# Two Strassen sums kept in PSUM over seven chunks, and another order of down products and up units

## The chip, the cores and the metric

The kernel runs on one core of one Trainium2 chip. The metric is the device time of one execution in microseconds (us), the median of the runs shown; the profile is of one further execution. TensorE does the matmuls, VectorE (DVE) and ScalarE (ACT) the elementwise work, GpSimd (POOL) and SyncE (SP) mostly issue DMAs.

## The reference

A hybrid decoder block over 256 tokens of width 2048 in float32: an mLSTM branch and a block-sparse attention branch from one projection, merged by gates, then a residual and a squared-ReLU MLP. The change touches only the MLP:

```python
hn = rmsnorm(x, norm_ffn_pre[l])
u = jnp.square(jax.nn.relu(jnp.einsum('bsd,df->bsf', hn, w_up[l])))   # 2048 -> 8192
y = jnp.einsum('bsf,fd->bsd', u, w_down[l])                           # 8192 -> 2048
x = x + rmsnorm(y, norm_ffn_post[l])
```

## The kernel before

**Splitting.** TensorE multiplies rounded float32 (`float32r`). Each weight unit (128x2048, 1 MB) is loaded and split into a high part `whi` (a ScalarE cast, line 169) and a remainder `wlo` (a DVE subtraction, line 170), in two halves of 128x1024. Four buffers of each exist, so two units. A product is three matmuls: high by high, high by low, low by high.

**The MLP.** The hidden width 8192 is taken in eight chunks (`NCH = 8`, j = 0 to 7) of 1024. An *up unit* (U, `up_step`, product `mm_feat_one`, lines 215 to 217) makes 128 hidden channels with 48 matmuls of 256 columns; `up_post` (line 760 and a square on ScalarE) evacuates it. Eight U fill a chunk. For the chunks 0 to 6 the down projection goes by Strassen-Winograd products: `group(j, p)` takes one half p of the output columns with seven *down products* (D, `mm_factor`, lines 226 to 232, 12 matmuls of 512 columns) named p1, q5, p6, p2, q7, q3, q4, always in this order. A chunk thus has 14 D, and between them stand the eight U of the next chunk. The order is the string in the diff, written by hand.

**What a D needs.** Its right factor is a weight block or a sum of blocks. For q5, p6 and q4 DVE forms a running sum of 128x2048 first (lines 859, 865 and 881) from blocks `r11, r12, r22, r21`; for q7 a GpSimd DMA adds r22 onto r12 (line 874). The sums live in the four `rawl` buffers, up units and r11 in the three `raw` buffers, all loaded by SP's queue in order. The left factor is a sum or difference of quarters of the hidden activations; `factors(j)` makes seven `xs` from them (lines 776, 777, 787, 792, 796, 800), four after the chunk's last U and one after each of the next three D.

**What a D leaves.** Its PSUM bank is added into SBUF accumulators by DVE (`add`, line 849; line 900 for q7); in chunk 0 the first write of an accumulator is a ScalarE copy (line 847). `v` takes p1 and p6; `y11`, `y12`, `y21`, `y22` take the others. Bank "a" holds p1, and p2 is accumulated on top of it; q3 goes on top of q5 in "e", q4 on top of q7 in "b"; p6 has "f". After chunk 6, `v` is combined into the y's (line 896). Five banks rotate for U and D (`acc_tile`), three others (`sm_tile`) serve small matmuls outside this stage.

**Steps.** The main loop writes the split of step i before the matmuls and the post of step i-1. A scheduler of the framework then fixes each engine's instruction order from its own timing estimates, and within an engine the order is static. Chunk 7 is done afterwards without Strassen (`down_step`, `hold_step`, `last_step`).

Of the kernel before, what the change touches and what calls it, by code (L numbers as in the profile page):

```python
# [19 lines left out]
ALU = mybir.AluOpType  # L20
# [15 lines left out]
NCH = DFF // FCH  # L36
# [49 lines left out]
def tile_hybrid_block(ctx, tc, xT, pos, pre, small, wa, wi, wo, wu, wd, wpost, out):  # L86
    nc = tc.nc
    V, S, G, PE = nc.vector, nc.scalar, nc.gpsimd, nc.tensor
# [17 lines left out]
    def acc_tile():  # L106
        return pacc.tile([P, 512], F32, name="acc", tag="acc")

    def sm_tile():
        return psm.tile([P, 512], F32, name="sm", tag="sm")  # L110
# [39 lines left out]
    def load(src):  # L150
        raw = raw_tile()
        nc.sync.dma_start(out=raw[:, 0:src.shape[1]], in_=src)
        return raw

    def split(raw, place=None, half=1024, pieces=1, between=None):
        parts = []
        for h in range(2):
            if place is None:
                hi = wp.tile([P, 1024], F32R, name="whi", tag="whi", bufs=4)
                lo = wp.tile([P, 1024], F32R, name="wlo", tag="wlo", bufs=4)  # L160
            else:
                hi, lo = place[:, h, 0], place[:, h, 1]
            n = half // pieces
            for i in range(pieces):
                if between:
                    between(h * pieces + i)
                s = slice(i * n, (i + 1) * n)
                r = raw[:, h * half + i * n:h * half + (i + 1) * n]
                S.copy(out=hi[:, s], in_=r)  # L169
                V.tensor_tensor(out=lo[:, s], in0=r, in1=hi[:, s].bitcast(F32), op=ALU.subtract)  # L170
            parts.append((hi, lo))
        return parts

    def wk(parts, k, n):
        per = 8 if n == P else 2
        hi, lo = parts[k // per]
        s = slice((k % per) * n, (k % per + 1) * n)
        return hi[:, s], lo[:, s]
# [42 lines left out]
    def mm_factor(acc, parts, f, start, stop, pinned=False, more=False):  # L221


        for k in range(4):
            hi, lo = wk(parts, k, 512)
            first = PE.matmul(out=acc, lhsT=f[:, k, 0], rhs=hi, start=start and k == 0,  # L226
                              stop=False, skip_group_check=more)
            if pinned:
                tc.keep_in_program_order(first)
            PE.matmul(out=acc, lhsT=f[:, k, 1], rhs=hi, start=False, stop=False,  # L230
                      skip_group_check=more)
            PE.matmul(out=acc, lhsT=f[:, k, 0], rhs=lo, start=False, stop=stop and k == 3,  # L232
                      skip_group_check=more)
# [433 lines left out]
    late = {}  # L667
# [88 lines left out]
    uh, xs, todo = {}, {}, []  # L756
# [73 lines left out]
    def wd_unit(j, e, v):  # L830
        return wd[8 * j + 2 * e + v]

    def long_raw():
        return pool["f"].tile([P, 2048], F32, name="rawl", tag="rawl", bufs=4)

    def group(j, p):

        e1, e2 = 2 * p, 2 * p + 1
        b11, b12, b21, b22 = (wd_unit(j, e, v) for v in range(2) for e in (e1, e2))
        y, v = late["y"], late["v"][:, p]  # L840
        y11, y12, y21, y22 = (y[:, h, e * 512:(e + 1) * 512] for h in range(2) for e in (e1, e2))
        r, acc = {}, {}

        def add(dst, a, op=ALU.add):
            if j == 0 and op == ALU.add and id(dst) not in seen:
                seen.add(id(dst))
                S.copy(out=dst, in_=a)
            else:
                V.tensor_tensor(out=dst, in0=dst, in1=a, op=op)
        seen = set()  # L850

        def w_b11():
            r["11"] = load(b11)
            return [split(r["11"])]

        def w_t1():
            r["12"], r["t"] = long_raw(), long_raw()
            nc.sync.dma_start(out=r["12"], in_=b12)
            V.tensor_tensor(out=r["t"], in0=r["11"], in1=r["12"], op=ALU.add)
            return [split(r["t"])]  # L860

        def w_t2():
            r["22"] = long_raw()
            nc.sync.dma_start(out=r["22"], in_=b22)
            V.tensor_tensor(out=r["t"], in0=r["t"], in1=r["22"], op=ALU.add)  # L865
            return [split(r["t"])]

        def w_b21():
            r["21"] = long_raw()
            nc.sync.dma_start(out=r["21"], in_=b21)  # L870
            return [split(r["21"])]

        def w_t3():
            nc.gpsimd.dma_start(out=r["12"], in_=b22, accum_op=ALU.add)
            return [split(r["12"])]

        def w_b22():
            return [split(r["22"])]

        def w_t4():  # L880
            V.tensor_tensor(out=r["t"], in0=r["t"], in1=r["21"], op=ALU.add)
            return [split(r["t"])]

        def step(name, w, bank, start, post):
            def mm(units):
                if start:
                    acc[bank] = acc_tile()
                mm_factor(acc[bank], units[0], xs[j, name], start, True, more=not start)

            def after():  # L890
                post(acc[bank])
                if todo:
                    todo.pop(0)()
                if j == NCH - 2 and name == "q4":
                    for dst, op in ((y12, ALU.subtract), (y21, ALU.add), (y22, ALU.subtract)):
                        V.tensor_tensor(out=dst, in0=dst, in1=v, op=op)
            return w, mm, after

        def q7(a):
            V.tensor_tensor(out=y22, in0=y22, in1=a, op=ALU.subtract)  # L900
        return [step("p1", w_b11, "a", True, lambda a: add(v, a)),
                step("q5", w_t1, "e", True, lambda a: add(y22, a)),
                step("p6", w_t2, "f", True, lambda a: add(v, a)),
                step("p2", w_b21, "a", False, lambda a: add(y11, a)),
                step("q7", w_t3, "b", True, q7),
                step("q3", w_b22, "e", False, lambda a: add(y12, a)),
                step("q4", w_t4, "b", False, lambda a: add(y21, a))]
# [79 lines left out]
    def up_step(j, i):  # L987
        feat_step(wu[8 * j + i], hmov, lambda a: up_post(j, i, a), product=mm_feat_one)

    def down_group(j, p):  # L990

        made = []

        def part(n, what):
            def f(*a):
                if not made:
                    made.extend(group(j, p))
                x = made[n][what]
                if what == 0:
                    return x() if callable(x) else [split(load(u)) for u in x]  # L1000
                return x(*a)
            return f
        return [(part(n, 0), part(n, 1), part(n, 2)) for n in range(7)]
# [6 lines left out]
        up_step(0, i)  # L1010
    for j in range(NCH - 1):
        downs, i = down_group(j, 0) + down_group(j, 1), 0
        for what in "DUDUDDUDUDDUDUDDUDUDDD":
            if what == "D":
                steps.append(downs.pop(0))
            else:
                up_step(j + 1, i)
                i += 1
# [24 lines left out]
    units = {}  # L1043
# [100 lines left out]
```

## Time and profile before

| | before |
|---|---|
| median of 3 runs | 1436.42 us (1435.86 to 1437.91) |
| the profiled execution | 1436.87 us, span 1435.1 us |
| TensorE, DVE, ScalarE busy | 98%, 80%, 57% of the span |
| TensorE's granted clock | 0.997 of full speed |

The span goes from the first to the last instruction of the profile. A busy share says how much of it an engine executed; the ends of matmuls are modelled, so consecutive ones overlap in the records. An idle time is put down to the instruction whose semaphore came last.

### The profile page before, as it was taken

The page shows a single profiled execution, that of the slowest core. Times are in us where ns is not written, and L with a number is a line of the kernel's source. Part 1 is how long each engine was busy: PE and PEld are TensorE (multiplying, and loading weights), DVE is VectorE, ACT ScalarE, POOL GpSimd, SP SyncE. Part 2 cuts the span into 40 slices and gives each one's busy share as a digit, 9 for nine tenths or more (in the row PEclk, how much of TensorE's full clock was granted, in tenths as well). Part 3 has the DMA queues.
Part 4 walks back from the last instruction along what each step waited for, and adds up shares of the span by engine and source line. Part 5 has one row for each costly group of instructions (what it writes and reads, how often), then busy time and mean ns, then how long its engine had stood idle before and what let it go on. Part 6 is the DMA issues. An engine that isn't in the chain of part 4 may idle for free.

```text
span 1435.1 us, 21795 instructions
## 1 busy us (share of the span) xinstructions
PE 1410.6 (98%) x8570; PEld 1251.7 (87%) x8570; DVE 1147.5 (80%) x1607; ACT 815.2 (57%) x1200; POOL 17.3 (1%) x31
## 2 busy tenths in 40 slices
PE   8999999999999999999999999999999999999997
PEld 7988888888888888888899989989889898888975
DVE  7777766777676666665687899998999989999985
ACT  7655555565554445555656665565655655565561
POOL 0000000000000000000000000000000000000000
PEclk9999999999999999999999999999999999999998
DMA  8654444544455455554627665657646667655651
GB/s 255 222 182 176 162 171 178 184 177 174 175 184 198 178 190 190 180 202 176 249 77 251 236 217 171 261 185 262 232 152 239 225 209 246 216 195 195 239 201 59
DMA packets 44455, 282.45 MB, mean 197 GB/s; under 512 B 5116, under 2 KB 7424, under 8 KB 11712
## 3 DMA queue, kind: packets, MB, share of 16 engines
q1 hardware_dynamic: 41904, 265.57, 50.0%
q0 software_dynamic: 2304, 15.47, 5.8%
q8 instruction: 67, 1.10, 0.3%
q14 instruction: 36, 0.29, 0.1%
q10 hardware_dynamic: 144, 0.01, 0.0%
HBM read 278.93 MB, written 2.10 MB: 196 GB/s over the span
## 4 chain that ended last, share of the span: by engine, by line
PE 84%; DVE 11%; issue 2%; DMA 2%; ACT 1%; SPq 0%; DVEq 0%; ACTq 0%
PE acc L188 27%; PE acc L189 14%; PE acc L217 7%; PE acc L215 7%; PE acc L216 7%; DVE wlo L170 5%; PE acc L232 5%; PE acc L226 5%; PE acc L230 5%; PE acc L200 2%; PE acc L205 2%; DMA raw<-in_wa_dram 2%; PE acc L204 2%; DVE xs L777 1%; DVE rawl L865 1%
## 5 line engine op out<-in xcount | busy, mean ns | idle before, releaser
L169 ACT CAST whi<-raw 128x1024 fp32r<-128x1024 f32 (+2 forms) x420 | 424.9, 1016 | 418.9 <-PE acc L188 173.8
L170 DVE TENSOR_TENSOR wlo<-raw,whi 128x1024 fp32r<-128x1024 f32 (+2 forms) x420 | 495.2, 1182 | 207.2 <-ACT whi L169 197.5
L188 PE MATMUL acc<-xw,whi 128*128 128x512 f32 x1152 | 408.3, 395 | 0.0
L189 PE MATMUL acc<-xw,wlo 128*128 128x256 f32 x1152 | 328.6, 285 | 0.0
L217 PE MATMUL acc<-hw,wlo 128*128 128x256 f32 x992 | 279.7, 283 | 4.9 <-DVE wlo L170 4.9
L216 PE MATMUL acc<-hw,whi 128*128 128x256 f32 x992 | 279.0, 282 | 0.0
L215 PE MATMUL acc<-hw,whi 128*128 128x256 f32 x992 | 277.8, 282 | 0.0
L188 PEld LDWEIGHTS acc<-xw,whi 128*128 128x128 f32 x1152 | 216.4, 188 | 49.0 <-issue 0.4
L169 ACT CAST whi<-rawl 128x1024 fp32r<-128x1024 f32 x168 | 173.5, 1048 | 116.8 <-PE acc L216 52.1
L189 PEld LDWEIGHTS acc<-xw,wlo 128*128 128x128 f32 x1152 | 216.6, 188 | 0.9
L170 DVE TENSOR_TENSOR wlo<-rawl,whi 128x1024 fp32r<-128x1024 f32 x168 | 201.8, 1219 | 8.0 <-ACT whi L169 6.4
L217 PEld LDWEIGHTS acc<-hw,wlo 128*128 128x128 f32 x992 | 186.9, 188 | 9.9 <-DVE wlo L170 7.3
L215 PEld LDWEIGHTS acc<-hw,whi 128*128 128x128 f32 x992 | 186.0, 188 | 4.6 <-DVE t L760 0.2
L216 PEld LDWEIGHTS acc<-hw,whi 128*128 128x128 f32 x992 | 186.9, 188 | 2.0
L226 PE MATMUL acc<-whi,xs 128*128 128x512 f32 x440 | 174.7, 397 | 2.9 <-ACT whi L169 2.7
L232 PE MATMUL acc<-wlo,xs 128*128 128x512 f32 x440 | 172.3, 396 | 1.8 <-DVE wlo L170 1.8
L230 PE MATMUL acc<-whi,xs 128*128 128x512 f32 x440 | 173.9, 396 | 0.0
L232 PEld LDWEIGHTS acc<-wlo,xs 128*128 128x128 f32 x440 | 82.7, 188 | 20.9 <-DVE wlo L170 4.6
L226 PEld LDWEIGHTS acc<-whi,xs 128*128 128x128 f32 x440 | 82.7, 188 | 20.7 <-ACT whi L169 6.1
L230 PEld LDWEIGHTS acc<-whi,xs 128*128 128x128 f32 x440 | 82.7, 188 | 18.1
L188 PE MATMUL acc<-mg,whi 128*128 128x512 f32 x240 | 84.2, 393 | 0.0
L189 PE MATMUL acc<-mg,wlo 128*128 128x256 f32 x240 | 67.7, 283 | 0.0
(258 smaller groups left out, 1618.5 us busy)
## 6 DMA issues: line engine op xcount, KB each, us to landing
raw<-in_wi_dram SPq DMA_DIRECT2D x96, 1024.0 KB, 4.8
raw<-in_wu_dram SPq DMA_DIRECT2D x64, 1024.0 KB, 6.2
rawl<-in_wd_dram SPq DMA_DIRECT2D x42, 1024.0 KB, 8.2
raw<-in_wd_dram SPq DMA_DIRECT2D x22, 1024.0 KB, 4.9
raw<-in_wo_dram SPq DMA_DIRECT2D x16, 1024.0 KB, 4.8
rawl<-in_wd_dram POOLq DMA_DIRECT2D x14, 1024.0 KB, 10.7
raw<-in_wa_dram SPq DMA_DIRECT2D x8, 520.0 KB, 4.7
raw<-in_wa_dram SPq DMA_DIRECT2D x16, 256.0 KB, 5.0
```

The source lines that it names most:

```text
L169: S.copy(out=hi[:, s], in_=r)
L170: V.tensor_tensor(out=lo[:, s], in0=r, in1=hi[:, s].bitcast(F32), op=ALU.subtract)
L188: PE.matmul(out=accs[i][:, 0:2 * T], lhsT=hi, rhs=m, start=k == 0, stop=False)
L189: PE.matmul(out=accs[i][:, 0:T], lhsT=lo, rhs=m[:, 0, :], start=False, stop=k == nk - 1)
L200: first = PE.matmul(out=acc, lhsT=m[:, 0, ts], rhs=hi, start=start and k == 0, stop=False)
L204: PE.matmul(out=acc, lhsT=m[:, 1, ts], rhs=hi, start=False, stop=False)
L215: PE.matmul(out=acc, lhsT=hi, rhs=m[:, 0, :], start=k == 0, stop=False)
L216: PE.matmul(out=acc, lhsT=hi, rhs=m[:, 1, :], start=False, stop=False)
L217: PE.matmul(out=acc, lhsT=lo, rhs=m[:, 0, :], start=False, stop=k == KT - 1)
L226: first = PE.matmul(out=acc, lhsT=f[:, k, 0], rhs=hi, start=start and k == 0, stop=False, skip_group_check=more)
L230: PE.matmul(out=acc, lhsT=f[:, k, 1], rhs=hi, start=False, stop=False, skip_group_check=more)
L232: PE.matmul(out=acc, lhsT=f[:, k, 0], rhs=lo, start=False, stop=stop and k == 3, skip_group_check=more)
```

## The change

The products p1 and p6 get a PSUM bank per column half that is held from chunk 0 to chunk 6 and accumulates all seven products: three `sm_tile` banks and one `acc_tile` bank. Their additions into `v` go. In chunk 6 p1's bank is copied to `v`, and after p6 `v` is added to `y11` and p6's bank to `v`. p2 starts its own bank. The order string becomes another one with the same 14 D and 8 U.

```diff
         def step(name, w, bank, start, post):
             def mm(units):
+                if bank in ("p1", "p6"):
+
+                    if j == 0:
+                        late[bank, p] = sm_tile() if (bank, p) != ("p6", 1) else acc_tile()
+                    acc[bank] = late[bank, p]
+                    mm_factor(acc[bank], units[0], xs[j, name], j == 0, True, more=j > 0)
+                    return
                 if start:
                     acc[bank] = acc_tile()
                 mm_factor(acc[bank], units[0], xs[j, name], start, True, more=not start)
...
+        def last_p1(a):
+            if j == NCH - 2:
+                S.copy(out=v, in_=a)
+
+        def last_p6(a):
+            if j == NCH - 2:
+                V.tensor_tensor(out=y11, in0=y11, in1=v, op=ALU.add)
+                V.tensor_tensor(out=v, in0=v, in1=a, op=ALU.add)
+
         def q7(a):
             V.tensor_tensor(out=y22, in0=y22, in1=a, op=ALU.subtract)
-        return [step("p1", w_b11, "a", True, lambda a: add(v, a)),
+        return [step("p1", w_b11, "p1", True, last_p1),
                 step("q5", w_t1, "e", True, lambda a: add(y22, a)),
-                step("p6", w_t2, "f", True, lambda a: add(v, a)),
-                step("p2", w_b21, "a", False, lambda a: add(y11, a)),
+                step("p6", w_t2, "p6", True, last_p6),
+                step("p2", w_b21, "a", True, lambda a: add(y11, a)),
                 step("q7", w_t3, "b", True, q7),
...
-        for what in "DUDUDDUDUDDUDUDDUDUDDD":
+        for what in "DUDDUDUDDUDUDDUDUDDUDD":
```

## Rows read from the trace of the kernel before

**Rows 1.** The page, busy time of each engine, share of the span, instructions.
```profile
PE 1410.6 (98%) x8570; PEld 1251.7 (87%) x8570; DVE 1147.5 (80%) x1607; ACT 815.2 (57%) x1200; POOL 17.3 (1%) x31
```

**Rows 2.** Busy time by stretch, two MLP chunks; then granted clock, DMA share, GB/s.
```profile
945.00:1032.00 87.00, 85.58 (x554) 77.01 (x553) 82.12 (x84) 51.36 (x60) 1.71 (x2) 1.00 0.63 218
1119.00:1206.00 87.00, 85.59 (x554) 77.01 (x553) 82.12 (x84) 51.37 (x60) 1.72 (x2) 1.00 0.64 219
```

**Rows 3.** Waits from 900 to 1400: total us, times, longest.
```profile
ACT whi L169 <- DVE rawl L865: 38.4, 11, 4.0
...
PE acc L217 <- DVE wlo L170: 4.9, 5, 1.0
...
PE acc L226 <- ACT whi L169: 2.2, 5, 0.4
PE acc L232 <- DVE wlo L170: 1.8, 2, 1.3
```

**Rows 4.** Groups by line and form, 900 to 1400, then the tile `v`.
```profile
L170 DVE TENSOR_TENSOR wlo<-rawl,whi 128x1024 fp32r<-128x1024 f32 x132 | 158.6, 1219 | 6.4 <-ACT whi L169 4.8
L169 ACT CAST whi<-rawl 128x1024 fp32r<-128x1024 f32 x132 | 136.3, 1048 | 90.9 <-PE acc L216 38.7 <-DVE rawl L865 38.4 <-PE acc L230 10.1
L865 DVE TENSOR_TENSOR rawl<-rawl 128x2048 f32<-128x2048 f32 x11 | 25.1, 2285 | 0.0
L859 DVE TENSOR_TENSOR rawl<-raw,rawl 128x2048 f32<-128x2048 f32 x10 | 22.9, 2292 | 4.8 <-DMA raw<-in_wd_dram 4.1 <-DMA rawl<-in_wd_dram 0.6
L849 DVE TENSOR_TENSOR v<-v,acc x26: 675/680/685, 795.4 to 1359.0; 128x512 f32<-128x512 f32 x26
```

**Rows 5.** TensorE's timeline, 1052 to 1062: start, duration, line, idle before.
```profile
1052.10 0.40 PE L230 MATMUL acc<-whi,xs 128*128 128x512 f32 x1
...
1054.21 0.39 PE L230 MATMUL acc<-whi,xs 128*128 128x512 f32 x1
1055.57 0.39 PE L217 MATMUL acc<-hw,wlo 128*128 128x256 f32 x1 [0.97 <-DVE wlo L170]
1055.80 0.28 PE L215 MATMUL acc<-hw,whi 128*128 128x256 f32 x1
...
1061.02 0.28 PE L217 MATMUL acc<-hw,wlo 128*128 128x256 f32 x1
```

**Rows 6.** DVE's timeline over one chunk, 1052 to 1140.
```profile
1052.09 2.29 DVE L881 TENSOR_TENSOR rawl<-rawl 128x2048 f32<-128x2048 f32 x1
1054.30 1.22 DVE L170 TENSOR_TENSOR wlo<-raw,whi 128x1024 fp32r<-128x1024 f32 x1
...
1086.53 2.29 DVE L865 TENSOR_TENSOR rawl<-rawl 128x2048 f32<-128x2048 f32 x1
1089.24 0.42 DVE L760 SCALAR_TENSOR_TENSOR t<-acc,rbc 128x256 f32<-128x256 f32 x1 [0.43 <-PE acc L217]
1090.00 2.36 DVE L170 TENSOR_TENSOR wlo<-rawl,whi 128x1024 fp32r<-128x1024 f32 x2 [0.34 <-ACT whi L169]
...
1094.01 2.28 DVE L881 TENSOR_TENSOR rawl<-rawl 128x2048 f32<-128x2048 f32 x1
...
1106.15 2.29 DVE L859 TENSOR_TENSOR rawl<-raw,rawl 128x2048 f32<-128x2048 f32 x1
...
1109.50 0.42 DVE L760 SCALAR_TENSOR_TENSOR t<-acc,rbc 128x256 f32<-128x256 f32 x1
...
1125.91 1.22 DVE L170 TENSOR_TENSOR wlo<-rawl,whi 128x1024 fp32r<-128x1024 f32 x1
1127.05 0.69 DVE L800 TENSOR_TENSOR s_b<-s_b,u 128x512 f32<-128x512 f32 x1
...
1130.25 2.29 DVE L865 TENSOR_TENSOR rawl<-rawl 128x2048 f32<-128x2048 f32 x1
...
1139.13 2.29 DVE L881 TENSOR_TENSOR rawl<-rawl 128x2048 f32<-128x2048 f32 x1
```

**Rows 7.** Waits from 770 to 936, chunk 0 and most of chunk 1.
```profile
PE acc L226 <- ACT whi L169: 0.5, 2, 0.3
```

## The prediction

> **What bounds the kernel now.** I read the page first. TensorE is busy 98% of the span, VectorE (DVE) 80%, ScalarE 57% [rows 1], so the question is what little TensorE idles and where. The stretches of one MLP chunk each come next: in both shown TensorE is busy 85.6 of 87.0 us and DVE 82.1 [rows 2], at a granted clock of 1.00. So two engines are nearly full here, with DVE's share far above its mean. The waits between 900 and 1400 us say who keeps TensorE waiting: always a weight half that is not yet split, by DVE's `wlo` or ScalarE's `whi`, never a PSUM bank [rows 3]. I also note there how long ScalarE waits for the sum of line 865: 38.4 us in 11 times [rows 3].
>
> The reader should see a pipeline with little slack. A weight unit passes a cast (ScalarE), a subtract (DVE) and the matmuls, and only four halves (two units) of `whi` and `wlo` exist. DVE can thus be little more than one unit ahead of TensorE.
>
> **The floor.** In the PE timeline nine steps between starts of 512-column matmuls take 2.11 us, 0.234 each; 44 steps between 256-column ones take 5.22 us, 0.119 each [rows 5]. A down product (D, 12 matmuls) is 2.81 us, an up unit (U, 48) 5.69, a chunk (14 D, 8 U) 84.9. The same instruction (line 881, p = 0) starts at 1052.09 and 1139.13 [rows 6], a period of 87.04. So 2.1 us per chunk are lost, in two places: 1.0 us of idle before a U's `wlo` and 0.4 before a D's `whi`, five times each [rows 3], plus their shadows (an idle of 0.97 is a start 1.13 late, since the records' modelled ends overlap [rows 5]). Five chunks lose 10.7, the first two some 0.8 (0.5 of idle, [rows 7]), the end of the last chunk 2.1 (1.8 of idle at line 232, [rows 3]): 13.6 us. No better feeding of TensorE in this stage can give more.
>
> **The change part by part.**
>
> *Fewer sums.* The 26 DVE additions into `v` go [rows 4]; at 0.68 us each with 0.08 of overlap to the next, 0.60, that is 15.6 us. Added, both halves p together: two copies on ScalarE in place of the two that started `v`, and four DVE additions at 0.60. Net 13.2 us of DVE, 2.4 in each of chunks 1 to 5. This alone ends nothing: DVE isn't what TensorE waits for everywhere, only around two places. What counts is which of the additions stand ahead of a late weight. Of the p1 sum, one of p = 0 does (between `wlo` halves after the chunk's border), so 0.6 us is won there. For TensorE nothing changes: p2 starts a bank of its own instead of adding to p1's, in the same 12 matmuls. Held for seven chunks are the three spare banks and one of five rotating ones. The a, e, b banks and a U's are then the four in use; since no TensorE wait names a bank now [rows 3], I price this at nothing, with an upper bound under the rivals. ScalarE's count stays, in copies of the same size, at 57% busy [rows 1].
>
> *The order.* D and U counts stay. Before: D U D U DD U D U DD U D U DD U D U DDD, after: D U DD U D U DD U D U DD U D U DD U DD. At the border four D in a row become three. But p = 0's q5 and p6, which had a U between them, now stand side by side, right after that border (q3 q4 p1 U q5 p6). Both take a 2048-wide sum before they can be split (lines 859, 865: 2.3 us, [rows 4]). No DMA is added; loads move with their steps, and on SP's queue the ones of p6 and U swap.
>
> *What goes.* The 1.24 late at p = 0's U (idle 0.97 and shadows, [rows 5]) comes from line 881's sum, which stands ahead of that U's `wlo` (1052.09, then 1054.30, [rows 6]) while p6 and p2 were side by side. Afterwards p6 is followed by a U, whose cast is ready early, so I take this to go. The border's loss, the 0.9 left of the 2.1, falls with one D less in the run: 0.3 in my estimate, between 0 and 0.9.
>
> *What comes: the pair.* I count from the end of the chunk's last U (U7), which is the row of line 760 at 1109.50 before [rows 6]. TensorE then has q3, q4, p1 (8.4), U0 (5.7) and q5 (2.8): p6 starts at 16.9 and needs its first `wlo` 0.5 later, at 17.4. DVE, at that point, has split q3 and half of q4; line 881's sum of p = 1 and line 859's of the next chunk are done, as they were before (1094.01 and 1106.15, [rows 6]). DVE has left, start to start (0.08 below the durations, [rows 4, 6]): the U's own 0.33, a half of q4 1.13, p1, U0 and q5 2.27 each, two drains 1.2, and the seven 0.6 us operations of the factors which before's order put between 1109.50 and q5's second half at 1125.91 [rows 6]. Sum 13.7. Next before came a factor difference (line 800, 1127.05): 14.3. Then line 865 starts; from its start to the first subtract of its unit is 3.47 us where DVE was not in the way (1086.53 to 1090.00, [rows 6]: the sum 2.3, the cast 1.05, [rows 4]), and that subtract is 1.2: ready at 18.9. TensorE is 1.5 late. As a check, the pair of p = 1 exists before: line 865 there starts 2.7 us ahead of its U's end (1086.53, 1089.24, [rows 6]) and nothing stalls, with 1.3 to spare (first half ready at 1091.2, used at 1092.5 by the floor). Here it starts 0.2 after the U's end, 2.9 later in relation to it: 1.6 late.
>
> The bounds of this term: if four factor operations that aren't urgent come behind line 865, it starts 2.4 earlier and the pair costs 0. If all factors and U0's post come ahead (1.5 more), it costs 3.0. If line 859's sum is not done in time, 2.2 more, 5.2. The factors come earlier in the written order than p6's sum, which speaks for the upper order; before's rows show two of them behind it, which speaks for the lower. I take the middle of 1.5 and 3.0: 2.2 us.
>
> *Sum.* Six chunks at 2.2 and the first (no D run ahead) at 1.8: 15.0; six borders at 0.3: 1.8; the end, with two D instead of three after the last U, 1.5 (0 to 2.5): together 18.3 against 13.6. The change costs 4.7 us. The profiled execution is 1436.87, its span 1435.1 and 1.8 around it; it stands 0.45 above the median of the runs. 1436.4 + 4.7 = 1441.1.
>
> **The Trainium skill** (Perfetto Trace Analysis, Identifying the Most-Contended Engine) holds that relieving the engine with the highest occupancy improves a kernel. The trace agrees in part: DVE has 82.1 of 87.0 here [rows 2], but TensorE's floor is higher. By that rule alone each chunk would shorten to the floor. Its result is the first rival, priced from rows below.
>
> **Rivals.**
>
> 1. *The pair is hidden, and the relief counts.* DVE reaches line 865 two microseconds before U0's end, as in p = 1. For it: 2.4 us less DVE work per chunk and two bubbles' causes gone. Against: the count above leaves DVE no idle time from the border to there. Left over: borders 1.8, end 1.5, some 0.2 per chunk for small lags, 4.7 in all; 8.9 won, 1427.5. It decides if the pair costs under 1.1.
>
> 2. *An even trade.* Before's order of the factors holds, the pair costs 1.5 (first chunk 1.2): 10.2 + 3.3 = 13.5 against 13.6, 1436.3. The additions then only gave DVE idle time, so the change's first half would have done nothing that the end sees.
>
> 3. *Line 859 slips too.* The sum for q5 needs a slot and a 1 MB load; with p2 and q7 side by side the slot comes free earlier, but DVE is fuller there. The pair at 4.4 costs 13 more than forecast: 1454. A PSUM wait belongs here as well: four rotating banks instead of five. If each chunk had one matmul group wait for two drains (1.2), that would be 8.4 us, 1449.5 with the rest. The Trainium skill (Perfetto Trace Analysis, Optimization Strategy) reads a bubble that repeats as a possible lack of SBUF or PSUM for the next tile. By the rows the present ones are named after weights, so I give banks little.
>
> **Chances.** The forecast case (1439.3 to 1449) has 0.38, rival 3 0.08, rival 2 0.24, rival 1 0.30. This kernel's measurement tells some 0.2%, 2.9 us, from no change. Slower 0.46, same 0.24, faster 0.30. The range takes in rival 1's price down to 1428 and the upper order with a bad end: 1428 to 1452. The forecast case alone: 1439 to 1449.
>
> **What would show it.** Right: in the steady chunks, TensorE's wait of about 1 us before line 217 is gone; a new one appears at p6 of p = 0, released by ScalarE's `whi` or DVE's `wlo`, ScalarE idle before it on line 865; the chunk's period is 87.4, DVE's busy time in a chunk 2.7 lower (79.4). The additions to `v` fall to two. Wrong, if the period drops towards 85, if line 865's row of p = 0 starts before U0's post, or if a TensorE row names a DVE addition (a bank).

## The result and the profile after

The changed kernel takes 1460.29 us (median of 4 runs, 1459.72 to 1463.63) beside 1436.14 for the kernel before in the same comparison: a ratio of 1.0172, 95% interval 1.0153 to 1.0191. It is slower by 24 us, where 4.7 were forecast and the range ended at 1452. Its profiled execution is 1460.17 us, the span 1458.4.

The page of the changed kernel, busy time of each engine and, in tenths over 40 slices, TensorE's granted clock:

```profile
PE 1423.2 (98%) x8570; PEld 1262.1 (87%) x8570; DVE 1137.2 (78%) x1585; ACT 814.4 (56%) x1200; POOL 17.3 (1%) x31
...
PEclk9999999999999999999999999999999999999999
```

DVE lost 22 instructions and 10 us of work against [rows 1], as the change says, and TensorE, with the same 8570 matmuls, is busy 12.6 us longer. That second number is the odd one: a late weight makes idle time, not busy time. The tenths of the clock line are too coarse to say why.

The waits of the changed kernel from 770 to 1440 us (total, times, longest):

```profile
ACT xs L776 <- DVE s_b L800: 28.0, 6, 5.2
...
PE sm L226 <- ACT whi L169: 16.0, 7, 3.0
...
ACT whi L169 <- DVE rawl L865: 8.0, 6, 2.4
...
PE sm L232 <- DVE wlo L170: 5.4, 7, 1.1
...
PE acc L232 <- DVE wlo L170: 0.8, 1, 0.8
```

The wait of line 217 is gone from the list, as is that of line 226 on an "acc" bank [rows 3]. Instead TensorE waits in a product on an "sm" bank, once per chunk, first for a high half (2.3 us each) and then for a low one (0.8). Idle put down to waits is 22.2 us against 9.4 before [rows 3, 7], 12.8 more. That is about half of the 24 us.

TensorE's timeline at the place, in the chunk around 1140:

```profile
1138.55 0.28 PE L217 MATMUL acc<-hw,wlo 128*128 128x256 f32 x1
1138.66 0.40 PE L232 MATMUL acc<-wlo,xs 128*128 128x512 f32 x1
...
1140.76 0.40 PE L232 MATMUL acc<-wlo,xs 128*128 128x512 f32 x1
1143.51 0.51 PE L226 MATMUL sm<-whi,xs 128*128 128x512 f32 x1 [2.35 <-ACT whi L169]
1143.85 0.39 PE L230 MATMUL sm<-whi,xs 128*128 128x512 f32 x1
1145.31 0.79 PE L232 MATMUL sm<-wlo,xs 128*128 128x512 f32 x1 [1.07 <-DVE wlo L170]
1145.90 0.63 PE L226 MATMUL sm<-whi,xs 128*128 128x512 f32 x1
...
1146.76 0.63 PE L232 MATMUL sm<-wlo,xs 128*128 128x512 f32 x1
```

U0's last matmul starts at 1138.55, q5's rest follows, then p6 of p = 0 waits twice: 2.52 us between starts beyond the usual 0.234, then 1.23; with the 0.11 between them p6 is 3.85 us late. After it the starts are 0.43 apart instead of 0.234, with no wait named. The same stretch by windows (time, then busy time of TensorE, its weight loads, DVE, ScalarE, GpSimd, then granted clock, DMA share and GB/s):

```profile
983.92:1075.47 91.55, 88.17 (x553) 79.29 (x553) 80.07 (x80) 51.26 (x60) 1.71 (x3) 0.96 0.60 207
...
1140.00:1145.40 5.40, 1.98 (x8) 0.97 (x7) 5.40 (x7) 4.27 (x7) 0.00 (x0) 0.97 0.05 20
1145.40:1147.00 1.60, 1.60 (x4) 1.31 (x5) 1.60 (x2) 0.91 (x2) 0.00 (x0) 0.50 0.00 0
1147.00:1149.00 2.00, 2.00 (x8) 1.62 (x8) 2.00 (x3) 1.04 (x1) 0.00 (x0) 0.64 0.00 0
1149.00:1153.00 4.00, 4.00 (x32) 3.82 (x31) 4.00 (x3) 1.50 (x2) 0.00 (x0) 1.00 0.71 262
```

The granted clock is 0.50, the lower level of 1.2 GHz, right after the wait, in which TensorE had been busy 1.98 of 5.40 us, and 1.00 again by 1149. That is the added busy time. The first row is a whole chunk, from one GpSimd DMA issue of p = 0 to the next: 91.55 us where 87.4 were forecast, with DVE at 80.07.

DVE's timeline, from line 859's sum and U7's post to p6's weights:

```profile
1117.46 2.28 DVE L859 TENSOR_TENSOR rawl<-raw,rawl 128x2048 f32<-128x2048 f32 x1
...
1124.81 0.42 DVE L760 SCALAR_TENSOR_TENSOR t<-acc,rbc 128x256 f32<-128x256 f32 x1
1125.74 1.23 DVE L170 TENSOR_TENSOR wlo<-rawl,whi 128x1024 fp32r<-128x1024 f32 x1 [0.51 <-ACT whi L169]
...
1139.10 0.68 DVE L800 TENSOR_TENSOR s_b<-s_b,u 128x512 f32<-128x512 f32 x1
1139.70 0.42 DVE L760 SCALAR_TENSOR_TENSOR t<-acc,rbc 128x256 f32<-128x256 f32 x1
1140.04 2.28 DVE L865 TENSOR_TENSOR rawl<-rawl 128x2048 f32<-128x2048 f32 x1
1142.24 0.68 DVE L849 TENSOR_TENSOR y<-y,acc 128x512 f32<-128x512 f32 x1
1142.84 0.68 DVE L777 TENSOR_TENSOR xs<-s_b,xs 128x512 fp32r<-128x512 f32 x1
1143.44 0.68 DVE L777 TENSOR_TENSOR xs<-u,xs 128x512 fp32r<-128x512 f32 x1
1144.04 2.35 DVE L170 TENSOR_TENSOR wlo<-rawl,whi 128x1024 fp32r<-128x1024 f32 x2
```

Line 865 starts 1.4 us after U0's end, TensorE arrives at p6 at 1141.0, and ScalarE's cast of p6 can begin only at 1142.4. Behind the sum stand three small operations, then the subtract. ScalarE's timeline of the same stretch:

```profile
1139.82 0.62 ACT L776 CAST xs<-s_b 128x512 fp32r<-128x512 f32 x1 [5.12 <-DVE s_b L800]
...
1142.41 1.99 ACT L169 CAST whi<-rawl 128x1024 fp32r<-128x1024 f32 x2 [1.13 <-DVE rawl L865]
```

ScalarE stands for 5 us at a copy that waits for line 800, with p6's casts queued behind it. This is a second candidate for what is late (rival E below), and it needs an experiment, since after its copies ScalarE waits another 1.13 us, for line 865.

### The profile page after: what moved, and what is told of

Same layout as the page of the kernel before. It is cut to its first block, busy times and chain, and to the rows that moved or that the text cites. A ratio compares the mean times of both kernels' runs of the same rounds, so it can differ in the third digit from the quotient of the medians.

```text
span 1458.4 us, 21829 instructions
## 1 busy us (share of the span) xinstructions
PE 1423.2 (98%) x8570; PEld 1262.1 (87%) x8570; DVE 1137.2 (78%) x1585; ACT 814.4 (56%) x1200; POOL 17.3 (1%) x31
## 4 chain that ended last, share of the span: by engine, by line
PE 89%; DVE 7%; issue 2%; ACT 1%; DMA 1%; SPq 0%; DVEq 0%; ACTq 0%
PE acc L188 26%; PE acc L189 14%; PE acc L215 8%; PE acc L216 8%; PE acc L217 8%; PE acc L230 5%; PE acc L226 5%; PE acc L232 5%; DVE wlo L170 3%; PE acc L200 2%; PE acc L205 2%; PE acc L204 2%; PE sm L232 1%; DVE xs L777 1%; PE sm L226 1%
## 5 line engine op out<-in xcount | busy, mean ns | idle before, releaser
L230 PE MATMUL acc<-whi,xs 128*128 128x512 f32 x356 | 140.9, 396 | 0.0
L226 PE MATMUL acc<-whi,xs 128*128 128x512 f32 x356 | 140.7, 396 | 0.0
L232 PE MATMUL acc<-wlo,xs 128*128 128x512 f32 x356 | 138.0, 395 | 0.8 <-DVE wlo L170 0.8
L232 PEld LDWEIGHTS acc<-wlo,xs 128*128 128x128 f32 x356 | 66.9, 188 | 14.5 <-DVE wlo L170 1.3
L230 PEld LDWEIGHTS acc<-whi,xs 128*128 128x128 f32 x356 | 67.0, 188 | 14.0
L226 PEld LDWEIGHTS acc<-whi,xs 128*128 128x128 f32 x356 | 67.1, 188 | 11.7
```

## The experiments

**Theories.** *A*: q5 and p6 of p = 0 stand side by side behind the chunk's border, so line 865's sum is late; TensorE waits there, and a lower clock follows. *B*: the held PSUM banks cost the time. *C*: runs of D must be spread evenly. *D*: the slow steps after the wait are late halves, not the clock. *E*: ScalarE's blocked queue, not line 865, is late.

Each kernel below was timed beside the kernel before on the same chip; the ratio's 95% interval is in brackets.

**The order alone** (the kernel before with the new string):

```diff
-        for what in "DUDUDDUDUDDUDUDDUDUDDD":
+        for what in "DUDDUDUDDUDUDDUDUDDUDD":
```

> The new order string alone, the sums as before. Theory A (p = 0's q5 and p6 side by side behind the chunk's border: line 865's sum comes too late, TensorE waits 3.9 us there, and a lower clock for some us follows): as slow as the changed kernel or slower, since the addition of p1 stands in the same stretch again, 1460 to 1480 us. Rival B (the held PSUM banks cost the time): 1434 to 1440 us.

Measured: 1452.33 us, 1.0113 [1.0098, 1.0129]. The order alone gives two thirds of the loss, so B's number falls. A's lower bound of 1460 was missed too. Its waits, TensorE's alone, 770 to 1400:

```profile
PE acc L226 <- ACT whi L169: 14.1, 7, 2.4
PE acc L232 <- DVE wlo L170: 4.2, 8, 0.8
```

The same place, seven times, a little shorter than with the whole change (18.3 us of idle in all, for 22.2). So in this order the held sums didn't help but cost 8 us more; the run on the factors' place below says through what.

**The sums alone** (the changed kernel with the old string).

> The sums kept in PSUM, the old order string. Theory A: no pair there, 2.4 us less DVE work per chunk, but only what stands ahead of a late weight counts: 1429 to 1436 us. Rival B (held banks): 1450 us or more, TensorE rows that wait for DVE additions.

Measured: 1432.82 us, 0.9979 [0.9969, 0.9989]: 3 us faster. None of TensorE's waits is put down to an addition that empties a bank:

```profile
PE acc L217 <- DVE wlo L170: 2.9, 5, 1.1
PE acc L232 <- DVE wlo L170: 1.8, 2, 1.3
PE acc L226 <- ACT whi L169: 0.5, 2, 0.3
```

The forecast said that only additions ahead of a late weight would count. They do: 10.5 us less of DVE busy time (1137.0 against 1147.5 [rows 1]) bought 3, and the waits fell from 9.4 [rows 3, 7] to 5.2.

**The pair apart** (the changed kernel, q5 and p6 of p = 0 parted by a U again, still three D at the border):

```diff
-        for what in "DUDDUDUDDUDUDDUDUDDUDD":
+        for what in "DUDUDDUDUDDUDDUDUDDUDD":
```

> The changed kernel with the string D U D U DD U D U DD U DD U D U DD U DD: q5 and p6 of p = 0 apart again, still three D at the border. Theory A: no wait at p6 of p = 0, no lower clock, a chunk of 85.5 to 87 us, 1428 to 1438 us. Rival C (fewer U between the D near the border, whichever products they are): still over 1450 us. Rival B: still over 1450 us.

Measured: 1432.28 us, 0.9978 [0.9968, 0.9987]. B and C fall: same sums, same evenness, 28 us less. The wait at a late low half of a U is back:

```profile
PE acc L217 <- DVE wlo L170: 4.2, 5, 0.9
PE sm L226 <- ACT whi L169: 2.4, 5, 0.9
```

**One U moved** (the kernel before; a U goes from between q5 and p6 of p = 0 to between p6 and p2; the border's four D stay):

```diff
-        for what in "DUDUDDUDUDDUDUDDUDUDDD":
+        for what in "DUDDUDUDUDDUDUDDUDUDDD":
```

> The kernel before with one U moved, from between q5 and p6 of p = 0 to behind p6 and p2's place (D U DD U D U D U ..., four D at the border as before). Theory A: the pair stalls behind a border that is fuller still, 1460 to 1485 us. Rivals B and C (banks; evenness of the order): 1434 to 1442 us.

Measured: 1462.98 us, 1.0193 [1.0178, 1.0208]. One U in another place, without any other part of the change, is enough for the whole loss. Its waits at p6 are mostly 2.0 and 1.1 us of idle.

**The wait filled** (the changed kernel; the useless matmuls go into p2's bank, which p2 then starts anew):

```diff
                 if bank in ("p1", "p6"):
+                    if name == "p6" and p == 0 and j > 0:
+                        acc["a"] = acc_tile()
+                        hw = late["hw"]
+                        for _ in range(16):
+                            tc.keep_in_program_order(
+                                PE.matmul(out=acc["a"], lhsT=hw[:, 0, 0, 0:P], rhs=hw[:, 1],
+                                          start=True, stop=True))
...
-                if start:
+                if start and not (name == "p2" and p == 0 and j > 0):
                     acc[bank] = acc_tile()
```

> The changed kernel with 16 useless matmuls of 512 columns ahead of p6's of p = 0 in chunks 1 to 6, written into p2's bank before p2 starts it. Theory A with the clock: they fill the 3.8 us in which TensorE would wait (16 x 0.234), the granted clock stays at 1.00, and only the slow steps behind the wait (2.2 to 2.9 us a chunk) go: 1443 to 1448 us, the wait itself not won back. Rival D (the slow steps are matmuls that wait for late halves): 1457 to 1463 us.

Measured: 1449.07 us, 1.0091 [1.0076, 1.0106], a little above the forecast's 1448: 96 more matmuls, 11.2 us less than the changed kernel. Its windows around the same p6, the 16 matmuls in the first:

```profile
1136.00:1140.20 4.20, 4.20 (x20) 3.43 (x19) 4.20 (x5) 3.07 (x6) 0.00 (x0) 1.00 0.01 4
1140.20:1143.00 2.80, 2.76 (x13) 2.00 (x12) 2.80 (x3) 2.71 (x3) 0.00 (x0) 1.00 0.00 0
```

The granted clock stays at 1.00 and the slow steps are gone though the halves come no sooner (p6's first subtract starts 5.4 us after U0's end, 5.5 in the changed kernel): D falls. The matmuls took about as long as the wait (16 x 0.234 = 3.7), so some 11 us are what the lower clock costs, nearly 2 a chunk, and 12.8 of more waiting with 11.2 of clock come to the 24. The wait in chunk 0 was not filled, and the lower level follows it in this run.

**The last two factors later** (the changed kernel; DVE's order pinned so that line 865 stands ahead of line 800, and the last two factors follow p6's split):

```diff
-            V.tensor_tensor(out=t[2], in0=t[2], in1=a12, op=ALU.add)
+            tc.keep_in_program_order(
+                V.tensor_tensor(out=t[2], in0=t[2], in1=a12, op=ALU.add))
...
-            V.tensor_tensor(out=r["t"], in0=r["t"], in1=r["22"], op=ALU.add)
+            t2 = V.tensor_tensor(out=r["t"], in0=r["t"], in1=r["22"], op=ALU.add)
+            if p == 0:
+                tc.keep_in_program_order(t2)
...
-                if todo:
+                if todo and (len(todo) == 3 or name in ("p6", "p2")):
                     todo.pop(0)()
```

> The changed kernel with the last two factors (line 800's difference and two subtractions of line 777) put behind p6's split in DVE's order. Theory A: line 865 starts 0.6 us sooner and the first subtract behind it 1.2 to 1.8 us sooner; the wait at p6 falls from 3.8 to between 1.5 and 2.7 us and the low clock after it gets shorter or goes: 1445 to 1454 us. Rival C (evenness of the order) and B (banks): 1457 to 1463 us.

Measured: 1450.74 us, 1.0104 [1.0089, 1.0120], 9.5 us less than the changed kernel. Its waits at p6, TensorE's alone:

```profile
PE sm L226 <- ACT whi L169: 12.4, 7, 2.3
PE sm L232 <- DVE wlo L170: 3.7, 7, 0.5
```

They fall from 21.4 to 16.1 us; the rest of the gain is TensorE's busy time, 1418.2 for 1423.2. The place of three operations of 0.6 us on DVE, and of the two copies on ScalarE that moved along, was thus worth 9.5 us, about 1.6 a chunk with the clock. No copy stands ahead of p6's cast on ScalarE now, and still the cast starts only when the sum (866 is line 865's) is done:

```profile
1138.98 1.99 ACT L169 CAST whi<-rawl 128x1024 fp32r<-128x1024 f32 x2 [1.78 <-DVE rawl L866]
```

So E's queue isn't what ends this wait. In the changed kernel the scheduler had put the three operations around line 865; in the run with the order alone line 800 starts at 1139.36, behind line 865 at 1137.16. I take this to be the 8 us between the order alone and the whole change; that all of it is this wasn't shown. By the two profiles 3.9 of the 8 are idle time (18.3 and 22.2 us) and 4.1 are TensorE's busy time (1419.1 and 1423.2), and the second part, the clock, doesn't follow from the wait's length alone (last section).

**Without the sum** (the changed kernel; for p = 0, p6 is split from r22 alone, and q4's sum lacks r22, so that part of the computation is left out):

```diff
+            if p == 0:
+                return [split(r["22"])]
             V.tensor_tensor(out=r["t"], in0=r["t"], in1=r["22"], op=ALU.add)
             return [split(r["t"])]
```

> The changed kernel without line 865's sum for p = 0: p6 is split from the block r22 itself, and q4's sum lacks r22 as well, so this part of the computation is left out. Theory A: the wait for the high half at p6 goes, the second half may come up to 1 us late, no low clock: 1430 to 1440 us. Rival E (what is late is ScalarE's queue: its copy of line 776 waits 5.1 us for line 800, with p6's casts behind it): a wait of over 1.2 us at p6 stays: 1445 us or more.

Measured: 1433.65 us, 0.9984 [0.9975, 0.9994]. The long wait and the low clock are gone, and the time is A's, not the 1445 us or more of E. But a wait of 1.6 us stays, as E had it (over 1.2), though for p2's high half and not p6's. DVE's timeline (883 is line 881's sum, for q4), TensorE's and ScalarE's, three fences:

```profile
1127.37 0.69 DVE L800 TENSOR_TENSOR s_b<-s_b,u 128x512 f32<-128x512 f32 x1
...
1128.31 2.29 DVE L883 TENSOR_TENSOR rawl<-rawl 128x2048 f32<-128x2048 f32 x1
1130.51 1.22 DVE L170 TENSOR_TENSOR wlo<-rawl,whi 128x1024 fp32r<-128x1024 f32 x1
```

```profile
1130.02 0.39 PE L230 MATMUL sm<-whi,xs 128*128 128x512 f32 x1
1131.97 0.50 PE L226 MATMUL acc<-whi,xs 128*128 128x512 f32 x1 [1.56 <-ACT whi L169]
...
1132.55 0.39 PE L232 MATMUL sm<-wlo,xs 128*128 128x512 f32 x1
```

```profile
1130.05 0.61 ACT L776 CAST xs<-u 128x512 fp32r<-128x512 f32 x1
...
1130.89 1.03 ACT L169 CAST whi<-rawl 128x1024 fp32r<-128x1024 f32 x1
```

The scheduler filled the free place with q4's sum, and p6's second low half now stands behind that (it is done at 1131.7). The row that waits is p2's: its first two matmuls stand ahead of p6's rest, and its high half is cast behind two copies of line 776 and U0's square, until 1131.9. So two late pieces meet here: again a 2.2 us sum ahead of a weight that no U covers, and ScalarE's queue. With p2's cast in time, line 232 could have started at 1131.75 instead of 1132.55, which puts ScalarE's share near 0.8 us; that is an estimate from these rows, not a run.

**Two U between q5 and p6** (the changed kernel), and the same string with the sums as before:

```diff
-        for what in "DUDDUDUDDUDUDDUDUDDUDD":
+        for what in "DUDUUDDUDDDUDDUDUDDUDD":
```

> The sums kept in PSUM with the string D U D UU DD U DDD U DD U D U DD U DD: two U stand between q5 and p6 of p = 0, three D in a row twice. Theory A (a sum of 128x2048 is only late where no U precedes its product after the border): faster than both kernels, 1424 to 1431 us. Rival C (runs of D must be spread evenly): slower than 1436 us.

> The kernel before with the string D U D UU DD U DDD U DD U D U DD U DD, the sums of p1 and p6 added by DVE as before. If the order alone gives the gain of the last run: 1427 to 1430 us. If the sums in PSUM carry a part of it (3 us, as they gave with the old order): 1430 to 1434 us.

Measured: 1427.68 us, 0.9942 [0.9928, 0.9957], with the held sums, and 1427.65 us, 0.9937 [0.9921, 0.9954], with the old ones. Both beat the kernel before by 8 to 9 us. C falls for good: this is a less even order, with three D in a row twice. The held sums add nothing to it. In the first of the two, TensorE's main wait up to 1400 is:

```profile
PE sm L226 <- ACT whi L169: 4.7, 6, 0.8
```

## Why the prediction was right and wrong

**The floor and the sums: right.** The additions were worth little: 3 us in the old order, none in the last one. No TensorE row waits for a bank, and DVE has 80.1 in a chunk of the changed kernel (82.1 before, 79.4 forecast). Only in the new order did the held sums cost anything, 8 us, probably by what the scheduler then put around line 865.

**What goes: right.** Line 217's wait is gone, and the border's.

**What comes, the pair: the mechanism right, its size wrong.** This is the step that failed: 2.2 us a chunk, with 5.2 as the outer bound, stood there for what is 3.85 between starts in the chunk shown (2.6 to 4.5 over the seven) plus nearly 2 of clock. Three terms on top of the count's 1.5 (before's order of the factors) make the first figure:

- TensorE came sooner. The scheduler had put two of q5's twelve matmuls inside U0, so p6 was reached 2.3 us after U0, not 2.8: 0.5.
- Line 865 came later, 1.4 us after U0's end, not 0.2: 1.2. The count left out 0.5 of DVE idle before 1125.74 and the post of U0, 0.33, and U0 ended 0.2 sooner than counted.
- Behind the sum three small operations stood ahead of the first subtract, which the check with p = 1's pair had free: 4.0 from its start to that subtract, not 3.47, so 0.5.
- With the 1.5, together 3.7, near the 3.85 measured.

Taking the middle of two orders was no help: the wait lies above both, 1.5 and 3.0.

**The clock: missing.** The prediction read 1.00 in before's rows and took it as given. Before's waits are 1.3 us at most. In the profile six of the seven new waits were followed by the lower level, and nearly half of the loss, 11 us, came from it. So an error of some 1.6 us in the wait became one of some 3.5 a chunk.

**The rivals.** Line 859 did not slip: its row stands at 1117.46, before U7's post. A bank wait never showed. The Trainium skill's rule on the most-contended engine (Perfetto Trace Analysis, Identifying the Most-Contended Engine) gives 3 us here when the order is left alone, and nothing with the last order. Relieving DVE was not what this kernel lacked; the order in which DVE's long sums meet TensorE's products was.

## What to carry to other kernels

In a pipeline that is full on two engines, count the work of the feeding engine between two fixed points of the consumer, and see which long operations lie ahead of a piece that nothing covers; totals of busy time told neither sign nor size here. When such a count gives a wait well above those of the trace, price what the consumer's clock does after it as well. One U in another place cost 27 us, and another order of the same eight U won 8 to 9; the work that was taken away won 3 at most.

## What the runs showed of the hardware

TensorE's granted clock was 0.50 after the p6 wait (2.35 and 1.07 us of idle, with two matmuls between) and 1.00 again some 3 us later in this chunk, though TensorE was the busiest engine of the kernel by far; where useless matmuls filled the wait it stayed at 1.00. The shorter double wait of the run with the factors later (1.75 and 0.53 us) was still followed by 0.50, as its window behind them shows:

```profile
1141.40:1143.00 1.60, 1.60 (x4) 1.31 (x5) 1.60 (x2) 1.47 (x2) 0.00 (x0) 0.50 0.00 0
```

In the run without the sum, the single wait of 1.56 us left it at 1.00:

```profile
1132.00:1134.00 2.00, 2.00 (x11) 1.73 (x12) 2.00 (x3) 0.56 (x1) 0.00 (x0) 1.00 0.00 0
```

The length of a wait alone does not decide it. The run with the order alone has the same double wait in two neighbouring chunks (2.01 or 2.02 and 0.53 us); the level stayed at 1.00 after the first and was 0.50 after the second:

```profile
1140.64 0.50 PE L226 MATMUL acc<-whi,xs 128*128 128x512 f32 x1 [2.01 <-ACT whi L169]
1228.60 0.51 PE L226 MATMUL acc<-whi,xs 128*128 128x512 f32 x1 [2.02 <-ACT whi L169]
```

```profile
1141.40:1143.00 1.60, 1.10 (x5) 0.92 (x6) 1.60 (x3) 1.60 (x3) 0.00 (x0) 1.00 0.00 0
1229.40:1231.00 1.60, 1.14 (x3) 0.95 (x4) 1.60 (x3) 1.60 (x3) 0.00 (x0) 0.50 0.00 0
```

Chunk 0's wait, 1.62 and some 0.54 us in five of the profiles, was followed by 0.50 in three of them (the order alone, the wait filled, the factors later) and not in two (the changed kernel, one U moved). What decides between equal waits is open, so the 11 us are the price in these runs and not a fixed price of a wait.

The Trainium skill (TensorE: Matmul & The Clock Gate, Loop structure matters more than you think) says that the loop nest determines whether matmuls stay at the high level, and shows a long DMA wait between them as the bad case. The rows agree in part: up to 1400 us the level fell only in runs that have the pair and line 865's sum, but after short waits for a weight's split, and not after each of them.
